# Outputs of four batches in one tile and one store, with loads eight batches ahead

## The chip, the cores and the metric

The kernel runs on one core of one Trainium2 chip. The metric is the time of one execution in device microseconds, as the median of several runs.

## The reference

```python
batch, dim_i, dim_j, dim_k = 32, 256, 512, 384
# x: (batch, dim_i, dim_j) float32, y: (batch, dim_j, dim_k) float32
np.einsum('bij,bjk->bik', x, y).astype(np.float32)
```

There are 32 independent products of a 256 x 512 matrix with a 512 x 384 matrix. For each batch x is 512 KB, y is 768 KB and the output is 384 KB.

## The kernel before

The kernel works through the batches one by one. `load(b)` issues two DMAs on the SyncE queue: x of the batch to `x_sb` (L52), where each of the 128 partitions gets two neighbouring rows of x, one run of 4 KB, and y to `y_sb` (L53), where each partition gets four neighbouring rows of y, one run of 6 KB. `compute(b)` casts y to fp16 in four pieces, two on ScalarE (L61) and two on VectorE (L63). TensorE transposes x in eight pieces of 128 x 128 against an identity (L69), and VectorE and ScalarE take them out of PSUM in fp16 (L71, L73). Eight matmuls of 128 x 128 by 128 x 384 then sum into two PSUM tiles (L82), which ScalarE and VectorE copy to the halves of `o_sb` (L91, L93). `store(b)` issues one DMA on the SyncE queue that writes `o_sb` to the output (L97): each partition holds two neighbouring rows, so it is one run of 3 KB per partition on either side.

The order on the SyncE queue is the order of the program: the loads of batches 0 to 5, and then, for each batch b, the two loads of batch b + 6 and the store of batch b. SyncE issues in that order, so a store that waits for its copies keeps the loads behind it back. Each DMA signals one of eight semaphores in turn, and an issue waits until the DMA eight places before it has landed; at most eight DMAs are in flight. The identity is made on GpSimd after the first two loads in program order. `x_pool` and `y_pool` have AHEAD + 3 = 9 buffers, `o_pool` has 8.

Of the kernel before, what the change touches and what calls it, by code (L numbers as in the profile page):

```python
# [1 line left out]

# [5 lines left out]


MM_DT = mybir.dt.float16  # L10
F32 = mybir.dt.float32
P = 128
AHEAD = 6


@with_exitstack
def kernel(
    ctx: ExitStack,
    tc: tile.TileContext,
    x: bass.AP,  # L20
    y: bass.AP,
    out: bass.AP,
):
    nc = tc.nc

    B, I, J = x.shape
    _, _, K = y.shape

    NI = I // P
    NJ = J // P  # L30

    const_pool = ctx.enter_context(tc.tile_pool(name="const", bufs=1))
    x_pool = ctx.enter_context(tc.tile_pool(name="x_pool", bufs=AHEAD + 3))
    y_pool = ctx.enter_context(tc.tile_pool(name="y_pool", bufs=AHEAD + 3))
    yr_pool = ctx.enter_context(tc.tile_pool(name="yr_pool", bufs=4))
    xt_pool = ctx.enter_context(tc.tile_pool(name="xt_pool", bufs=4))
    o_pool = ctx.enter_context(tc.tile_pool(name="o_pool", bufs=8))
    tpsum_pool = ctx.enter_context(tc.tile_pool(name="tpsum", bufs=4, space=bass.MemoryType.PSUM))
    opsum_pool = ctx.enter_context(tc.tile_pool(name="opsum", bufs=4, space=bass.MemoryType.PSUM))

    identity = const_pool.tile([P, P], F32)

    loaded = {}

    def load(b):


        x_sb = x_pool.tile([P, NI, J], F32, name="x_sb")
        y_sb = y_pool.tile([P, NJ, K], F32, name="y_sb")
        x_src = x[b].rearrange("(p r) j -> p r j", p=P)  # L50
        y_src = y[b].rearrange("(q t) k -> q t k", q=P)
        nc.sync.dma_start(out=x_sb, in_=x_src)  # L52
        nc.sync.dma_start(out=y_sb, in_=y_src)  # L53
        loaded[b] = x_sb, y_sb

    def compute(b):
        x_sb, y_sb = loaded.pop(b)
        y_r = yr_pool.tile([P, NJ, K], MM_DT, name="y_r")
        for t in range(NJ):
            if t % 2 == 0:  # L60
                nc.scalar.copy(y_r[:, t], y_sb[:, t])  # L61
            else:
                nc.vector.tensor_copy(y_r[:, t], y_sb[:, t])  # L63

        xt_sb = xt_pool.tile([P, NJ, NI, P], MM_DT, name="xt_sb")
        for t in range(NJ):
            t_ps = tpsum_pool.tile([P, NI, P], F32, name="t_ps")
            for r in range(NI):
                nc.tensor.transpose(t_ps[:, r], x_sb[:, r, t::NJ], identity)  # L69
            if t % 2 == 0:  # L70
                nc.vector.tensor_copy(xt_sb[:, t], t_ps)  # L71
            else:
                nc.scalar.copy(xt_sb[:, t], t_ps)  # L73

        o_sb = o_pool.tile([P, NI, K], F32, name="o_sb")
        o_ps = [
            opsum_pool.tile([P, K], F32, name=f"o_ps_{r}", tag="o_ps")
            for r in range(NI)
        ]
        for t in range(NJ):  # L80
            for r in range(NI):
                nc.tensor.matmul(  # L82
                    o_ps[r],
                    xt_sb[:, t, r],
                    y_r[:, t],
                    start=(t == 0),
                    stop=(t == NJ - 1),
                )
        for r in range(NI):
            if r % 2 == 0:  # L90
                nc.scalar.copy(o_sb[:, r, :], o_ps[r])  # L91
            else:
                nc.vector.tensor_copy(o_sb[:, r, :], o_ps[r])  # L93
        return o_sb

    def store(b, o_sb):
        nc.sync.dma_start(  # L97
            out=out[b].rearrange("(p r) k -> p r k", p=P), in_=o_sb
        )

    HEAD = 2
    load(0)
    load(1)
    make_identity(nc, identity)
    for b in range(HEAD, AHEAD):
        load(b)
    for b in range(B):
        if b + AHEAD < B:
            load(b + AHEAD)
        store(b, compute(b))  # L110


# [1 line left out]
_INS = ['x', 'y']  # L114
_OUTS = [((32, 256, 384), 'float32')]


# [23 lines left out]
```

## Time and profile before

| | |
|---|---|
| median of 8 runs | 137.18 us (137.09 to 137.43) |
| the profiled execution | 137.23 us, its span 135.5 us |
| busy: PE, PEld, DVE, ACT, POOL | 64%, 44%, 46%, 51%, 1% of the span |
| HBM read and written | 41.94 MB and 12.58 MB, 403 GB/s over the span |
| granted TensorE clock, mean | 0.98 |
| x load: DMAs, KB each, median us from issue to landing | 32, 512, 10.2 |
| y load | 32, 768, 11.2 |
| store | 32, 384, 10.9 |

PE is TensorE's matmul, PEld its weight load, DVE VectorE, ACT ScalarE, POOL GpSimd, and SP SyncE; SPq is SyncE's sequencer, which issues the DMAs. In the rows of 40 slices each digit is the busy share of one slice of 3.39 us in tenths. A line of the timeline gives the start in us, the busy time in us, the engine, the line of the kernel, the operation, what it writes and reads, the count, and in brackets the idle time before it and what ended it. A group's line gives busy us and mean ns of one, then the engine's idle time just before the group's instructions and what ended most of it.

### The profile page before, as it was taken

The page shows a single profiled execution, that of the slowest core. Times are in us where ns is not written, and L with a number is a line of the kernel's source. Part 1 is how long each engine was busy: PE and PEld are TensorE (multiplying, and loading weights), DVE is VectorE, ACT ScalarE, POOL GpSimd, SP SyncE. Part 2 cuts the span into 40 slices and gives each one's busy share as a digit, 9 for nine tenths or more (in the row PEclk, how much of TensorE's full clock was granted, in tenths as well). Part 3 has the DMA queues.
Part 4 walks back from the last instruction along what each step waited for, and adds up shares of the span by engine and source line. Part 5 has one row for each costly group of instructions (what it writes and reads, how often), then busy time and mean ns, then how long its engine had stood idle before and what let it go on. Part 6 is the DMA issues. An engine that isn't in the chain of part 4 may idle for free.

```text
span 135.5 us, 1733 instructions
## 1 busy us (share of the span) xinstructions
PE 86.8 (64%) x512; PEld 60.2 (44%) x512; DVE 62.7 (46%) x160; ACT 68.8 (51%) x161; POOL 0.7 (1%) x6
## 2 busy tenths in 40 slices
PE   0599777777576677555676565676565677565640
PEld 0458555554255455334454344454344454344410
DVE  0247555554155544446454456554446544446520
ACT  3246666663266544546454656454646454546520
POOL 2000000000000000000000000000000000000000
PEclk9999999999689999999999999999999999999997
DMA  4999999999999999999999999999999999999993
GB/s 158 423 416 418 418 414 387 413 417 412 420 422 422 415 417 419 421 417 422 426 415 419 416 426 420 423 420 413 421 423 423 412 419 420 421 418 427 410 379 132
DMA packets 13833, 54.64 MB, mean 403 GB/s; under 512 B 1536, under 2 KB 1536, under 8 KB 13824
## 3 DMA queue, kind: packets, MB, share of 16 engines
q1 hardware_dynamic: 13824, 54.53, 98.7%
q8 instruction: 4, 0.07, 0.2%
q14 instruction: 5, 0.04, 0.1%
HBM read 41.94 MB, written 12.58 MB: 403 GB/s over the span
## 4 chain that ended last, share of the span: by engine, by line
DMA 88%; PE 4%; ACT 2%; issue 1%; SPq 1%; DVE 0%; ACTq 0%
DMA out_dram<-o_sb 33%; DMA y_sb<-in_y_dram 33%; DMA x_sb<-in_x_dram 22%; PE o_ps L82 4%; ACT y_r L61 2%; ACT o_sb L91 1%; DVE o_sb L93 0%; SPq L53 0%; SPq L52 0%; ACTq L61 0%; SPq L97 0%
## 5 line engine op out<-in xcount | busy, mean ns | idle before, releaser
L82 PE MATMUL o_ps<-y_r,xt_sb 128*128 128x384 f16 x256 | 49.5, 337 | 35.3 <-ACT y_r L61 29.8
L82 PEld LDWEIGHTS <-xt_sb 128*128 128x128 f16 x256 | 25.3, 99 | 52.6 <-issue 36.6
L69 PE MATMUL t_ps<-identity,x_sb 128*128 128x128 f32 x256 | 39.3, 298 | 8.1 <-DMA x_sb<-in_x_dram 8.1
L69 PEld LDWEIGHTS t_ps<-identity,x_sb 128*128 128x128 f32 x256 | 35.1, 210 | 17.0 <-PE o_ps L82 12.0
L93 DVE COPY o_sb<-o_ps 128x384 f32<-128x384 f32 x32 | 17.8, 557 | 44.3 <-PE o_ps L82 44.3
L61 ACT CAST y_r<-y_sb 128x384 f16<-128x384 f32 x64 | 29.7, 510 | 13.2 <-DMA y_sb<-in_y_dram 13.1
L73 ACT CAST xt_sb<-t_ps 128x256 f16<-128x256 f32 x64 | 23.6, 372 | 17.7 <-PE t_ps L69 15.2
L91 ACT COPY o_sb<-o_ps 128x384 f32<-128x384 f32 x32 | 15.3, 478 | 30.1 <-PE o_ps L82 30.1
L63 DVE CAST y_r<-y_sb 128x384 f16<-128x384 f32 x64 | 20.0, 355 | 19.7 <-DMA y_sb<-in_y_dram 19.5
L71 DVE CAST xt_sb<-t_ps 128x256 f16<-128x256 f32 x64 | 26.3, 421 | 4.1 <-PE t_ps L69 3.3
L61 ACT ACT_TABLE_LOAD x1 | 1.3, 1283 | 0.7 <-PEq L125 0.7
masks.py:199 POOL TENSOR_SCALAR_AFFINE_SELECT identity<-identity 128x128 f32<-128x128 f32 x1 | 0.3, 292 | 0.1
masks.py:197 POOL MEMSET identity<- 128x128 f32 x1 | 0.2, 204 | 0.3 <-POOLq L125 0.3
L125 POOL MEMSET const-bfloat16-1.0<- 128x1 bf16 x1 | 0.1, 101 | 0.0
L125 POOL MEMSET const-uint8-127<- 128x1 uint8 x1 | 0.1, 101 | 0.0
L125 POOL MEMSET const-float32-0.0<- 128x1 f32 x1 | 0.1, 98 | 0.2 <-issue 0.2
L125 POOL MEMSET const-float32-1.0<- 128x1 f32 x1 | 0.1, 98 | 0.0
## 6 DMA issues: line engine op xcount, KB each, us to landing
y_sb<-in_y_dram SPq DMA_DIRECT2D x32, 768.0 KB, 11.2
x_sb<-in_x_dram SPq DMA_DIRECT2D x32, 512.0 KB, 10.2
out_dram<-o_sb SPq DMA_DIRECT2D x32, 384.0 KB, 10.9
```

The source lines that it names most:

```text
L61: nc.scalar.copy(y_r[:, t], y_sb[:, t])
L63: nc.vector.tensor_copy(y_r[:, t], y_sb[:, t])
L69: nc.tensor.transpose(t_ps[:, r], x_sb[:, r, t::NJ], identity)
L71: nc.vector.tensor_copy(xt_sb[:, t], t_ps)
L73: nc.scalar.copy(xt_sb[:, t], t_ps)
L82: nc.tensor.matmul(o_ps[r], xt_sb[:, t, r], y_r[:, t], start=(t == 0), stop=(t == NJ - 1),)
L91: nc.scalar.copy(o_sb[:, r, :], o_ps[r])
L93: nc.vector.tensor_copy(o_sb[:, r, :], o_ps[r])
L125: nc = _bacc.Bacc("TRN2", target_bir_lowering=False, num_devices=1)
```

## The change

The outputs of several batches in a row share one tile `o_sb` of 128 partitions x n batches x 768 values, with n from the list `GROUPS`: six groups of four, two of two and four of one. A group is stored by one DMA after its last batch. For n over 1 a new function `wide_dma` builds the DMA instruction itself, so that the two sides keep different shapes: on the side of SBUF one run per partition (12 KB for n = 4), on the side of HBM n runs of 3 KB, one in each batch of the output. AHEAD is 8 instead of 6, `x_pool` and `y_pool` have AHEAD + 2 = 10 buffers, and `o_pool` has four for the groups of four and two together and four for the single batches. The identity is made ahead of all loads in program order, and all first loads are issued in one loop. The computation of a batch is the same.

```diff
@@ -10,7 +10,32 @@
 MM_DT = mybir.dt.float16
 F32 = mybir.dt.float32
 P = 128
-AHEAD = 6
+AHEAD = 8
+GROUPS = [4, 4, 4, 4, 4, 4, 2, 2, 1, 1, 1, 1]
+
+
+def wide_dma(eng, out, in_):
+
+    nc = eng.bass
+
+    def side(ap):
+        return [
+            mybir.BassSymbolicTensorAccessPattern(
+                ap=ap.ap, dtype=ap.dtype, bass_ap=ap, is_dma=False
+            )
+        ]
+
+    return eng.add_instruction(
+        mybir.InstDMACopy(
+            name=nc.get_next_instruction_name(),
+            engine=eng.engine,
+            ins=side(in_),
+            outs=side(out),
+            queue="qSPDynamicHW",
+            mode="Copy",
+            cce_op=mybir.AluOpType.bypass,
+        )
+    )
 
 
 @with_exitstack
@@ -30,15 +55,16 @@
     NJ = J // P
 
     const_pool = ctx.enter_context(tc.tile_pool(name="const", bufs=1))
-    x_pool = ctx.enter_context(tc.tile_pool(name="x_pool", bufs=AHEAD + 3))
-    y_pool = ctx.enter_context(tc.tile_pool(name="y_pool", bufs=AHEAD + 3))
+    x_pool = ctx.enter_context(tc.tile_pool(name="x_pool", bufs=AHEAD + 2))
+    y_pool = ctx.enter_context(tc.tile_pool(name="y_pool", bufs=AHEAD + 2))
     yr_pool = ctx.enter_context(tc.tile_pool(name="yr_pool", bufs=4))
     xt_pool = ctx.enter_context(tc.tile_pool(name="xt_pool", bufs=4))
-    o_pool = ctx.enter_context(tc.tile_pool(name="o_pool", bufs=8))
+    o_pool = ctx.enter_context(tc.tile_pool(name="o_pool", bufs=4))
     tpsum_pool = ctx.enter_context(tc.tile_pool(name="tpsum", bufs=4, space=bass.MemoryType.PSUM))
     opsum_pool = ctx.enter_context(tc.tile_pool(name="opsum", bufs=4, space=bass.MemoryType.PSUM))
 
     identity = const_pool.tile([P, P], F32)
+    make_identity(nc, identity)
 
     loaded = {}
 
@@ -47,13 +73,11 @@
 
         x_sb = x_pool.tile([P, NI, J], F32, name="x_sb")
         y_sb = y_pool.tile([P, NJ, K], F32, name="y_sb")
-        x_src = x[b].rearrange("(p r) j -> p r j", p=P)
-        y_src = y[b].rearrange("(q t) k -> q t k", q=P)
-        nc.sync.dma_start(out=x_sb, in_=x_src)
-        nc.sync.dma_start(out=y_sb, in_=y_src)
+        nc.sync.dma_start(out=x_sb, in_=x[b].rearrange("(p r) j -> p r j", p=P))
+        nc.sync.dma_start(out=y_sb, in_=y[b].rearrange("(q t) k -> q t k", q=P))
         loaded[b] = x_sb, y_sb
 
-    def compute(b):
+    def compute(b, o_sb):
         x_sb, y_sb = loaded.pop(b)
         y_r = yr_pool.tile([P, NJ, K], MM_DT, name="y_r")
         for t in range(NJ):
@@ -72,7 +96,6 @@
             else:
                 nc.scalar.copy(xt_sb[:, t], t_ps)
 
-        o_sb = o_pool.tile([P, NI, K], F32, name="o_sb")
         o_ps = [
             opsum_pool.tile([P, K], F32, name=f"o_ps_{r}", tag="o_ps")
             for r in range(NI)
@@ -88,26 +111,30 @@
                 )
         for r in range(NI):
             if r % 2 == 0:
-                nc.scalar.copy(o_sb[:, r, :], o_ps[r])
+                nc.scalar.copy(o_sb[:, r], o_ps[r])
             else:
-                nc.vector.tensor_copy(o_sb[:, r, :], o_ps[r])
-        return o_sb
+                nc.vector.tensor_copy(o_sb[:, r], o_ps[r])
 
-    def store(b, o_sb):
-        nc.sync.dma_start(
-            out=out[b].rearrange("(p r) k -> p r k", p=P), in_=o_sb
-        )
+    def store(b, n, o_sb):
+        dst = out[b : b + n].rearrange("b (p r) k -> p b (r k)", p=P)
+        src = o_sb.rearrange("p b r k -> p b (r k)")
+        if n == 1:
+            nc.sync.dma_start(out=dst[:, 0], in_=src[:, 0])
+        else:
+            wide_dma(nc.sync, dst, src.rearrange("p (o b) q -> p o (b q)", o=1))
 
-    HEAD = 2
-    load(0)
-    load(1)
-    make_identity(nc, identity)
-    for b in range(HEAD, AHEAD):
+    for b in range(AHEAD):
         load(b)
-    for b in range(B):
-        if b + AHEAD < B:
-            load(b + AHEAD)
-        store(b, compute(b))
+    b = 0
+    for n in GROUPS:
+        o_sb = o_pool.tile([P, n, NI, K], F32, name="o_sb", tag=f"o_sb_{min(n, 2)}")
+        for g in range(n):
+            if b + AHEAD < B:
+                load(b + AHEAD)
+            compute(b, o_sb[:, g])
+            b += 1
+        store(b - n, n, o_sb)
+    assert b == B
 
 
 # ---- launch: one core; inputs and outputs as the reference has them ----
```

## The prediction

> **What bounds the kernel now.** I read the page first: the busy rows of the 40 slices, the queue table, the chain. Then the waits of the SyncE queue, then the timeline, and last the trace's records of single DMA packets and of landings (each DMA raises its semaphore sixteen times, once per engine).
>
> ```profile
> DMA  4999999999999999999999999999999999999993
> GB/s 158 423 416 418 418 414 387 413 417 412 420 422 422 415 417 419 421 417 422 426 415 419 416 426 420 423 420 413 421 423 423 412 419 420 421 418 427 410 379 132
> q1 hardware_dynamic: 13824, 54.53, 98.7%
> DMA 88%; PE 4%; ACT 2%; issue 1%; SPq 1%; DVE 0%; ACTq 0%
> L82 PE MATMUL o_ps<-y_r,xt_sb 128*128 128x384 f16 x256 | 49.5, 337 | 35.3 <-ACT y_r L61 29.8
> ```
>
> The sixteen DMA engines are busy from the second slice to the last but one, no compute engine passes 64%, and the chain is 88% DMA. So the time is a start of about 2 us, the service of 54.53 MB, and the last landing. Whatever doesn't alter what the DMA engines do per batch is worth nothing.
>
> The price of a batch comes from the SyncE timeline. Each issue waits for the DMA eight places before it, so it marks a landing.
>
> ```profile
> 9.31 0.33 SPq L53 DMA_DIRECT2D y_sb<-in_y_dram  x1
> ...
> 21.96 0.33 SPq L53 DMA_DIRECT2D y_sb<-in_y_dram  x1
> ...
> 81.76 0.34 SPq L97 DMA_DIRECT2D out_dram<-o_sb  x1
> ...
> 114.15 0.34 SPq L97 DMA_DIRECT2D out_dram<-o_sb  x1
> ```
>
> The issues at 9.31 and 21.96 waited for y of batches 1 and 5, with only loads moving: 12.65 / 4 = 3.16 us for the loads of a batch. From 81.76 to 114.15 eight batches passed with stores between loads: 32.39 / 8 = 4.05 us. A store among loads thus costs 4.05 - 3.16 = 0.89 us. At the end, with no loads left, the stores land on the slowest engine from 129.06 to 134.62: 5.56 / 6 = 0.93 us for a store among stores. So a store between loads hides 0.04 us of itself (0.041 unrounded) under its neighbours.
>
> The packet records give the fixed part. Their medians are 159 ns for a 4 KB run of x, 234 ns for 6 KB of y, 121 ns for 3 KB of the output and 9 ns for a semaphore write. 2 KB more cost 75 ns; take that slope from 159 and 9 ns remain, the price of the empty semaphore record too. A record is 9 ns plus 37.5 ns per KB. But records overlap: a store has 8 on each engine and a semaphore, 8 x 121 + 9 = 977 ns, and lands every 927. Of that 8 x 112.5 = 900 is bytes, so 27 ns over nine records, 3 ns each, is what the fixed part really costs when stores follow each other.
>
> **The change, part by part.**
>
> *Fewer records.* Six groups of four go from 512 read runs to 128, two groups of two from 256 to 128: 6 x 384 + 2 x 128 = 2,560 fewer, 160 on each engine. DMAs that store go from 32 to 12, so 20 semaphore writes fewer per engine: 180 records. No row shows a 12 KB read beside four 3 KB writes. The upper bound is the whole fixed part, 180 x 9 = 1.62 us saved; the lower bound is that the write side, which keeps its 3 KB pieces, sets the pace, and 20 x 3 ns = 0.06 us is saved. I take 3 ns, because it is measured between stores: 180 x 3 = 0.54 us saved.
>
> The Trainium skill (DMA: Bandwidth & Descriptors, "Why small descriptors are slow (HBM only)") speaks against the change: it puts a fixed overhead of about three cycles on a packet and says that joining descriptors is only worth it up to 256 B. The rows, 3 ns beside 116 ns of a 3 KB store run, leave the same little; by the rule taken strictly the saving would be 0 and the sum 138.0.
>
> *Fewer borders between loads and stores.* Before, 25 stores have loads behind them (stores 0 to 24); after, five blocks have (groups 0 to 4; the sixth store follows the last load). If the hidden 0.041 us belongs to a border, 20 of them are lost: 20 x 0.041 = 0.82 us. If it goes with the bytes, nothing is lost. I take 0.82: an engine's ring is served in order, so a load can only overlap the store next to it.
>
> The same page ("Where 436 GB/s comes from") gives a ceiling of 435 GB/s, 0.904 us for the bytes of one store. The row of 0.89 is already under that and the one of 0.93 just above; by the ceiling the 28 grouped stores could save 28 x 0.023 = 0.64 us at most, and the sum with the borders would be 137.4.
>
> *Loads eight ahead.* SyncE still waits for the DMA eight places back at each issue; in the changed program too the ninth DMA waits on the first's semaphore. So the depth in flight doesn't grow with AHEAD; only its bytes do, where a store is 1.5 MB. With the rings never empty, that is worth 0. A load now takes the buffer of ten batches before instead of nine; SyncE's wait for L69 was 0.7 us in total. The cover is the queue of seven DMAs, some 10 us; if it went, each late us would be a us of the end.
>
> *Stores moved back in SyncE's queue.* The first store comes after the loads of batch 11 instead of batch 6, and each grouped store waits for the copies of its fourth batch, with eight load issues of the next group behind it. Those copies must be done when the x load four batches later has landed. Compute, when its data is there, takes 3.28 us a batch:
>
> ```profile
> 17.09 1.46 PE L82 MATMUL o_ps<-y_r,xt_sb 128*128 128x384 f16 x8 [0.87 <-DVE y_r L63]
> ...
> 20.37 1.46 PE L82 MATMUL o_ps<-y_r,xt_sb 128*128 128x384 f16 x8 [0.87 <-DVE y_r L63]
> ...
> 35.26 1.12 PE L82 MATMUL o_ps<-y_r,xt_sb 128*128 128x384 f16 x3 [2.39 <-ACT y_r L61]
> ```
>
> Four batches compute in 13.1 us and arrive in 16.2. The third line is the risk: after 2.39 us of idle time eight matmuls ran at half the granted clock (the 6 in PEclk). A block of stores leaves PE idle up to 3.6 us, so each group may pay once; doubling one batch's 86.8 / 32 = 2.7 us still fits in the 3.1 us to spare. Cost 0. Built, PE, DVE, ACT and POOL hold the same instructions in the same order as before, the identity on POOL included. An issue of a wide store takes between 0.34 and, at four times the runs, 1.4 us of a queue that waits most of the time: 0.
>
> *The end.* Twelve batches of stores follow the last load, not seven, so the chain from last load through compute to last store (issue at 130.87, landing 134.6) is covered on every engine. Before, only the faster engines ran dry; the slowest landed a store every 0.93 us to the end. I take 0; the bound is the loss in slice 39, (420 - 379) / 420 x 3.39 = 0.33 us gained.
>
> **Sum.** -0.54 + 0.82 = +0.28 us on the profiled execution's 137.23 (135.5 span and 1.7 around it): 137.51. The median of the runs is 0.05 lower, so 137.45. Runs of this kernel spread so that 0.2%, 0.27 us, is what a measurement can tell; the forecast stands on that line. Own range 136.9 to 137.65: the overlap lost by half to wholly, the record at 2 to 4 ns (-0.31 to +0.46).
>
> **Rivals.**
>
> *Faster: the read run pays the whole fixed part.* Then 1.62 us go: 135.56, or 136.38 with the borders lost; I say 136.0. For it: all four sizes lie on one line with 9 ns, and 12 KB would be 459 ns instead of 4 x 121 = 484. Against it: the windows show a DMA share of 1.02 to 1.04, so records overlap, and 977 became 927. It decides where over 5 ns a record are saved.
>
> *Slower: the write side sets the pace.* Four 3 KB writes cost as four records did and the borders are lost: +0.82 - 0.06 = +0.76, 137.95. Long runs of loads may add: between 12 and 21 us, with loads alone, records rose to 162.4 and 238.6 ns on average, 8 x (3.4 + 4.6) = 64 ns a batch, though the landings kept 3.16 us; a sixth of that over 32 batches is 0.3 us, 138.25. It decides where less than 1.5 ns a record is saved.
>
> *The form doesn't do what it says.* If the queue cuts the read to 3 KB as well, the records stay and only borders and semaphores count: again 137.95.
>
> **How the numbers follow.** Forecast 0.40 (faster 0.05, same 0.20, slower 0.15), faster rival 0.32, slower rival 0.20 (0.02 of it same), uncut form 0.08. Faster 0.37, same 0.22, slower 0.41. The range leaves out the fullest saving, below 135.8, and the worst long runs, above 138.25.
>
> **What would show it.** On the page: the records of queue q1 fall from 13,824 by 2,560 + 320 to 10,944 if a wide run is one record; stay at 13,504 if not. Store to store on SyncE, a group's period before is 16.20 us. The forecast is 4 x 3.162 + 4 x 0.927 - 27 x 0.003 - 0.041 = 16.24, the faster rival's 15.95 to 16.08, the slower rival's 16.31. Wrong altogether would be SyncE waiting for ACT or DVE before a wide store, a DMA digit under 9 within the span, or a load period other than 3.16 us.

## The result and the profile after

The changed kernel takes 137.94 us (median of 12 runs, 137.76 to 138.4) where the kernel before takes 137.22 (35 runs): a ratio of 1.0053, 95% interval 1.0043 to 1.0064. It is slower by some 0.7 us. The profiled execution took 137.98 us with a span of 136.1.

The rows of the changed kernel's page that answer to those shown of before are these.

```profile
PEclk9999999999999975579999999999757999999975
DMA  4999999999999999999999999999999999999991
GB/s 169 413 418 421 416 416 416 412 406 418 410 436 398 418 418 416 439 402 424 416 415 434 412 418 411 415 435 406 422 416 431 415 414 418 409 430 415 413 383 61
q1 hardware_dynamic: 10944, 54.53, 97.9%
DMA 61%; PE 16%; DVE 10%; ACT 2%; SPq 2%; issue 1%; ACTq 0%
```

The DMA engines are still the bound: nines from the second slice to the last but one. The records of queue q1 fell to 10,944, the number that the prediction gave for one record per wide run, so the DMA does what its instruction says. The wide record has a median of 466 ns in the trace (the line of the other sizes gave 459). PEclk now drops twice within the run, for 10.2 and 6.8 us, each time behind a block of stores that had left TensorE idle (before, once for 3.4 us), and again at the end, where TensorE has no work left in either kernel; the DMA row stays at nine through it. The chain is of little use here: it ends at the last compute instruction, and the stores behind that have become longer.

The timeline of SyncE gives the pace of a group: the first load behind each wide store.

```profile
47.70 0.55 SPq L28 DMA_DIRECT2D out_dram<-o_sb  x1
49.60 0.34 SPq L76 DMA_DIRECT2D x_sb<-in_x_dram  x1
...
98.29 0.33 SPq L76 DMA_DIRECT2D x_sb<-in_x_dram  x1
```

From 49.60 to 98.29 three groups passed: 48.69 / 3 = 16.23 us each. The forecast was 16.24 (its own terms add up to 16.23), before it was 16.20. So the steady part costs 0.03 us a group, and that is not enough for the result. An issue of a wide store took 0.55 us of SyncE instead of 0.34.

None of the signs came by which the prediction would have been wrong altogether. The DMA digits stay at nine, and inside a group the loads of a batch still follow each other at 3.1 to 3.2 us (49.60 above, then 52.75 and 55.91). In front of each of its eight issues of wide stores SyncE waited for a load (us in total, times, longest):

```profile
SPq L28 <- DMA x_sb<-in_x_dram: 7.0, 7, 1.9
SPq L28 <- DMA y_sb<-in_y_dram: 1.3, 1, 1.3
```

The same list names a copy to `o_sb` (L114, L116) in front of none of them; only the fourth, at 80.58, went out 0.4 us after its wait for the load had ended.

The waits of SyncE show the second difference. The line of the closing waits of the kernel before comes first, that of the changed kernel after it (us in total, times, longest).

```profile
SPq L136 <- DMA out_dram<-o_sb: 3.2, 4, 0.9
```

```profile
SPq L163 <- DMA out_dram<-o_sb: 7.6, 1, 7.6
```

At its end SyncE waits for the eight DMA semaphores, in a fixed order. Before, the last store had the eighth of them (96 DMAs, a multiple of eight), and the last waits ended one by one as the last stores landed. After, the last store has the fourth (76 DMAs): SyncE stands 7.6 us in front of that one, and then still has four waits to go through that have long been fulfilled. In the trace these follow the last landing (135.04) at steps of 0.066 us. From the last landing to the end of the span there are 1.09 us, where before there were 0.83.

### The profile page after: what moved, and what is told of

Its sections match the earlier page's. It is cut to its first block, busy times and chain, and to the rows that moved or that the text cites. A ratio compares the mean times of both kernels' runs of the same rounds, so it can differ in the third digit from the quotient of the medians.

```text
span 136.1 us, 1658 instructions
## 1 busy us (share of the span) xinstructions
PE 87.6 (64%) x512; PEld 63.8 (47%) x512; DVE 57.9 (43%) x160; ACT 66.6 (49%) x161; POOL 0.7 (1%) x6
## 3 DMA queue, kind: packets, MB, share of 16 engines
q1 hardware_dynamic: 10944, 54.53, 97.9%
## 4 chain that ended last, share of the span: by engine, by line
DMA 61%; PE 16%; DVE 10%; ACT 2%; SPq 2%; issue 1%; ACTq 0%
DMA y_sb<-in_y_dram 40%; DMA x_sb<-in_x_dram 21%; PE o_ps L105 13%; DVE xt_sb L95 5%; DVE y_r L87 4%; PE t_ps L93 4%; ACT y_r L85 1%; SPq L76 1%; DVE o_sb L116 1%; SPq L77 1%; ACT xt_sb L97 1%; ACT o_sb L114 0%; ACTq L85 0%
## 5 line engine op out<-in xcount | busy, mean ns | idle before, releaser
L105 PE MATMUL o_ps<-y_r,xt_sb 128*128 128x384 f16 x256 | 52.1, 350 | 27.4 <-DVE y_r L87 18.3
L105 PEld LDWEIGHTS <-xt_sb 128*128 128x128 f16 x256 | 26.2, 103 | 46.7 <-issue 28.9
L93 PE MATMUL t_ps<-identity,x_sb 128*128 128x128 f32 x256 | 40.5, 307 | 11.4 <-DMA x_sb<-in_x_dram 11.4
L93 PEld LDWEIGHTS t_ps<-identity,x_sb 128*128 128x128 f32 x256 | 37.7, 210 | 15.6 <-issue 12.1
L116 DVE COPY o_sb<-o_ps 128x384 f32<-128x384 f32 x32 | 17.8, 557 | 49.8 <-PE o_ps L105 49.8
L114 ACT COPY o_sb<-o_ps 128x384 f32<-128x384 f32 x32 | 15.3, 478 | 32.4 <-PE o_ps L105 32.4
L95 DVE CAST xt_sb<-t_ps 128x256 f16<-128x256 f32 x64 | 24.7, 416 | 9.0 <-PE t_ps L93 8.9
```

The costliest lines, as they stand in the source:

```text
L105: nc.tensor.matmul(o_ps[r], xt_sb[:, t, r], y_r[:, t], start=(t == 0), stop=(t == NJ - 1),)
L114: nc.scalar.copy(o_sb[:, r], o_ps[r])
L116: nc.vector.tensor_copy(o_sb[:, r], o_ps[r])
```

## The experiments

The first theory was the prediction's: each border between stores and loads that is lost costs 0.04 us, a run that isn't read on its own saves some ns, nothing else counts. Its rivals were the depth of the loads, the wide form itself, and, after the first four runs, the closing waits. Each kernel's time is a median; ratios are to the kernel before on the same chip.

**Loads eight ahead, stores as before.**

```diff
-GROUPS = [4, 4, 4, 4, 4, 4, 2, 2, 1, 1, 1, 1]
+GROUPS = [1] * 32
-    o_pool = ctx.enter_context(tc.tile_pool(name="o_pool", bufs=4))
+    o_pool = ctx.enter_context(tc.tile_pool(name="o_pool", bufs=8))
```

> Stores of single batches as before (32 DMAs of 384 KB), but loads eight ahead, ten load buffers and the identity ahead of the loads, as in the changed kernel. Theory of the borders (each border between a store and loads that is lost costs 0.04 us, nothing else counts): 24 stores have loads behind them instead of 25, so 137.25 us, a batch every 4.05 us. Theory of the depth (loads eight ahead are what costs): 137.9 us, as the changed kernel. Theory of the wide form (a DMA of 1.5 MB or its 12 KB runs cost): 137.2 us.

Measured 137.31 us, ratio 1.0002 (0.9990 to 1.0015). The depth, the buffers and the place of the identity cost nothing that can be measured. The whole loss lies in the grouped stores and in what comes with them, fewer DMAs included. (Of the stores in this kernel 23 have loads behind them, not 24 as expected; by the theory that is 0.04 us.)

**Groups of four, but 3 KB runs on both sides.**

```diff
-            wide_dma(nc.sync, dst, src.rearrange("p (o b) q -> p o (b q)", o=1))
+            nc.sync.dma_start(out=dst, in_=src)
```

> The changed kernel with the same groups and one DMA per group, but cut to 3 KB runs on the side of SBUF too. Theory of the borders with the pace set by bytes and the write side: the read run is worth nothing, 137.95 us, a block of four lands in 3.7 us, as with 12 KB runs. Theory that 12 KB runs save their share (3 ns a record, 24 records a block): 0.07 us a block slower than the changed kernel, 138.4 us in all. Theory that 12 KB runs themselves are slow (466 ns a record where the line gave 459): 0.05 us a block faster, 137.6 us.

Measured 138.55 us, ratio 1.0085 (1.0063 to 1.0107). This is slower than the changed kernel by 0.6 us in the medians, 0.4 by the two ratios. So the wide run does save, which the theory of the write side had excluded. The two intervals just touch; the landings below give the same size.

**Groups of four, four stores one behind the other.**

```diff
-            wide_dma(nc.sync, dst, src.rearrange("p (o b) q -> p o (b q)", o=1))
+            for g in range(n):
+                nc.sync.dma_start(out=dst[:, g], in_=src[:, g])
```

> The changed kernel with the same groups in one tile, but each batch of a group stored by its own DMA, all of a group one behind the other after its last batch. Theory of the borders: as the changed kernel plus 20 semaphore writes, 137.95 to 138.1 us. Theory of the size (one DMA of 1.5 MB among the eight in flight, or its form, costs): back to 137.2 us.

Measured 138.51 us, ratio 1.0089 (1.0066 to 1.0111). Putting the stores of four batches behind one another costs 1.2 us against single stores (137.31), with the very same DMAs. It is not the size of a DMA. Nor did the DMA engines run dry behind stores that wait for compute: this kernel's DMA row has nines from the second slice to the last but one.

**Wide groups, loads six ahead.**

```diff
-AHEAD = 8
+AHEAD = 6
```

(with nine load buffers)

> The changed kernel with loads six ahead and nine load buffers. Theory of the borders: six blocks have loads behind them instead of five, 137.9 us. Theory of the depth: 137.2 us, as before.

Measured 138.14 us, ratio 1.0072 (1.0045 to 1.0099): not the depth, again.

The traces of these kernels split the loss. The landing of the last store is an increment for each of sixteen engines; its mean and its last tell what an average engine had to do, and how far the slowest was behind.

| kernel | mean engine's last landing, us | slowest behind the mean, us | last landing to end of span, us |
|---|---|---|---|
| single stores, eight ahead | 133.30 | 1.15 | 0.83 |
| four stores behind one another | 134.10 | 1.68 | 0.83 |
| one DMA, 3 KB runs | 134.08 | 1.66 | 1.09 |
| the changed kernel | 133.43 | 1.61 | 1.09 |

Grouping costs the mean engine 0.80 us. Twenty semaphore writes fewer save it 0.02, the wide runs 0.65. On top of that the slowest engine is 0.5 us further behind in the three kernels that group, and the closing waits add 0.26 where the last store is not on the last semaphore. (These are single executions; that of the single stores was 0.25 us under its median. In the kernel before and in the wide groups with loads six ahead, the faster engines wait for the last store at the end, so their means don't compare.)

The packet records show where the 0.80 sits. With four stores behind one another a record of x took 162.3 ns on average, one of y 237.7 and one of the output 121.8; with single stores 161.15, 236.1 and 121.4. An engine has 256 of each (4,096 by sixteen), which makes 0.31, 0.41 and 0.09 us: nine tenths of the loss is in the records of the loads and not of the stores. In the prediction's window with loads alone they were as long (162.4 and 238.6).

The 0.5 us is the difference of one execution of each kernel. Read while all engines still have work, at about 130 us, the slowest engine is 1.6 to 1.9 us behind in every trace with groups of four stored in a row and in that of the groups of two, and 1.0 to 1.5 with single stores, halves or quarters between the loads; the kernel before has 1.4 there, and the groups of eight, whose DMA engines run dry a little later, 1.2. So the direction holds, and the size is uncertain.

**Four small DMAs more, in the changed kernel and in the one before.** In each, behind the loads of batch 1:

```diff
+    pad = const_pool.tile([1, 4], F32, name="pad")
+    for i in range(4):
+        nc.sync.dma_start(out=pad[0:1, i : i + 1], in_=x[0, 0:1, i : i + 1])
```

> The changed kernel with four more DMAs of 4 bytes each, behind the loads of batch 1, so that the count of DMAs is 80 instead of 76 and the last store uses the last of the eight semaphores. In the runs so far SyncE ends by waiting for the eight semaphores in their fixed order; where the last store is on the fourth, four more waits of 0.066 us follow its landing (0.27 us), where it is on the eighth, none. Theory of the closing waits: 137.7 us, 0.25 less than the changed kernel, and one wait behind the last landing. Theory that all of the loss is in the service of the DMA engines: 137.95 us.

> The kernel before with the same four small DMAs: 100 DMAs instead of 96, the last store on the fourth semaphore. Theory of the closing waits: 137.5 us, 0.27 more than before, with five waits behind the last landing. Rival: 137.25 us.

Measured 137.83 us (1.0046, 1.0034 to 1.0058) and 137.77 us (1.0039, 1.0026 to 1.0052). The last landing came 0.17 us later in the one and 0.28 in the other. With the closing waits that makes 0.17 - 0.26 = -0.09 us for the changed kernel (the medians: -0.11, not to be told from nothing by the intervals) and 0.28 + 0.26 = 0.54 for the kernel before (the medians: 0.52). Whether the later landing is the price of the small DMAs was not tried by itself. The place where it belongs shows it whole: from the last landing to the end of the span the changed kernel with 80 DMAs has 0.83 us instead of 1.09, the kernel before with 100 DMAs 1.09 instead of 0.83. The closing wait of the latter now reads like that of the changed kernel:

```profile
SPq L139 <- DMA out_dram<-o_sb: 3.4, 1, 3.4
```

**12 KB runs on both sides.**

```diff
-            wide_dma(nc.sync, dst, src.rearrange("p (o b) q -> p o (b q)", o=1))
+            flat = out[b : b + n].rearrange("b i k -> (b i k)")
+            nc.sync.dma_start(
+                out=flat.rearrange("(p q) -> p q", p=P),
+                in_=src.rearrange("p b q -> p (b q)"),
+            )
```

> The changed kernel with stores whose runs are 12 KB on both sides: each partition's 12 KB goes to one run of the output, so the values lie elsewhere in it; bytes, groups and borders are the same. From cutting the read side to 3 KB the kernel lost 0.6 us. Theory that the fixed part is paid for each run that is read, whatever the write: 137.95 us, as the changed kernel, a block of four in 3.7 us. Theory that the written runs pay too: about 0.6 us less, 137.3 us. For the sum of the prediction, which put the fixed part on the read side: 137.95 us.

Measured 137.84 us, ratio 1.0039 (1.0025 to 1.0052), 0.1 less than with 3 KB writes; the two intervals overlap. In the traces the mean engine's last landing came 0.21 us earlier than in the changed kernel (133.22), where the wide read had gained 0.65, and a record of 12 KB took 460 ns (median) instead of 466. So most of the fixed part is paid on the read side; the times alone don't show that the written runs pay at all.

**Stores in two halves, one between the x load and the y load** (in the kernel before).

```diff
         nc.sync.dma_start(out=x_sb, in_=x_src)
+        if between is not None:
+            store(*between, 1)
...
+        dst = out[b].rearrange("(p two r) k -> two p r k", two=2, r=NI)
+        nc.sync.dma_start(out=dst[half], in_=o_sb[half:P:2])
```

> The kernel before with each store cut into two DMAs, of the even and of the odd partitions: one goes out behind the two loads, the other between the x load and the y load of the next step. Records and bytes are as before, 32 semaphore writes an engine more, and the blocks of stores between loads are doubled from 25 to 50. Theory of the borders (0.06 us for each block lost, from the runs so far): 25 x 0.06 = 1.5 us gained, 32 x 0.01 lost, 136.1 us, a batch every 4.0 us. Theory that it is the grouping in itself and not the border that costs: 137.2 + 0.3 = 137.5 us. If 64 partitions are read more slowly: 138 us and more.

Measured 137.05 us, ratio 0.9988 (0.9979 to 0.9997). An expectation that failed: it gained 0.2 us, not 1.1. A batch took 4.05 us as before (landings of the first halves on the slowest engine). So a border has no fixed price: 25 more of them, at the cost of 32 more semaphore writes, gave next to nothing. Why was not tried.

**Groups of two.**

```diff
-GROUPS = [4, 4, 4, 4, 4, 4, 2, 2, 1, 1, 1, 1]
+GROUPS = [2] * 12 + [4, 2, 1, 1]
```

> The changed kernel with groups of two (the last eight batches 4, 2, 1, 1), 80 DMAs, so no waits behind the last landing. Against single stores eight ahead (137.31 us), by the runs so far: theory of an even price for each store that is joined (grouping 0.06 lost, DMA 0.012 and run 0.03 saved): 12 x 0.06 - 16 x 0.042 = +0.05, 137.35 us. Theory that any grouping brings the late engines a fixed loss of some 0.8 us: 137.31 + 0.8 + 12 x 0.02 - 0.67 = 137.7 us.

Measured 137.15 us, ratio 0.9996 (0.9984 to 1.0008): no difference. The fixed loss of 0.8 us for any grouping is out; the even price gave 137.35, so twelve borders fewer cost less than that. (Its one profiled execution took 137.63, almost 0.5 us over the median, so its mean landing is not set beside the others.)

**Groups of eight.**

```diff
-GROUPS = [4, 4, 4, 4, 4, 4, 2, 2, 1, 1, 1, 1]
+GROUPS = [8, 8, 8, 2, 2, 2, 1, 1]
-    o_pool = ctx.enter_context(tc.tile_pool(name="o_pool", bufs=4))
+    o_pool = ctx.enter_context(tc.tile_pool(name="o_pool", bufs=2))
```

> The changed kernel with groups of eight (24 KB runs read), then 2, 2, 2, 1, 1: 72 DMAs, no waits behind the last landing. Even price: 22 blocks between loads less than with single stores, 22 x 0.06 - 24 x 0.042 = +0.3, 137.6 us. Fixed loss: 137.31 + 0.8 + 22 x 0.02 - 1.0 = 137.55 us. Theory that the length of the runs of loads is what costs: 138.2 us or more.

Measured 141.61 us, ratio 1.0321 (1.0300 to 1.0343), and none of the theories: it is another mechanism.

```profile
DMA  4999999999999999989999999989999999995556
```

```profile
SPq L28 <- DVE o_sb L116: 21.5, 2, 17.4
```

The DMA row falls to fives at the end, and SyncE stood 17.4 us before a wide store whose copies were not done. The likely reason, not tried by itself, is that with two output buffers the small last groups share their slots with the large ones and wait for their landing, so that compute ran late. The wait came behind the last load, whose issue was at 107.50, with nothing but stores left in the queue. So it says nothing on the length of the runs of loads; it shows what it costs when the DMA engines do run dry.

**Stores alone.** No loads and no arithmetic; a tile of zeros is stored to the 32 batches in four forms.

```diff
+    for b in range(8):
+        narrow(b)
+    wide(8); wide(12)
+    fused(16); fused(20)
+    both(24); both(28)
```

> No loads and no arithmetic: a tile of zeros is stored to the 32 batches, eight narrow stores, two wide ones of four batches, two of four batches with 3 KB runs on both sides, two with 12 KB runs on both sides. It measures the prices by themselves. By the prediction's terms, per four batches: narrow 4 x 0.927 = 3.71 us, one DMA with 3 KB runs 3.70, wide 3.63 (24 records at 3 ns less), both sides wide the same. Theory that joined runs save nothing where stores follow stores: 3.70 for all.

Landings on the slowest engine, per four batches: narrow 4.00 us (seven stores in 7.01), one DMA with 3 KB runs 3.91, wide 3.78, both sides wide 3.71. By these means each step of joining saves something, the wide run 0.12 us over 24 records, 5 ns each. But there are two landings of each joined form, and the two of one form lie up to 0.15 us apart (wide 3.86 and 3.71), so only the order is to be read from them. A narrow store alone took 1.00 us, more than the 0.89 among loads; its record was 124 ns instead of 121.

**12 KB runs, but the stores spread between the loads.** Each group of four is stored in four DMAs of every fourth partition, one behind the loads of each of the next four batches.

```diff
-GROUPS = [4, 4, 4, 4, 4, 4, 2, 2, 1, 1, 1, 1]
+GROUPS = [4] * 7 + [3, 1]
...
+    def store_part(b, n, o_sb, j):
+        dst = out[b : b + n].rearrange("b (p four r) k -> four p b (r k)", four=4, r=NI)
+        src = o_sb[j:P:4].rearrange("p b r k -> p (b r k)")
+        wide_dma(nc.sync, dst[j], src.rearrange("p (o q) -> p o q", o=1))
...
                 load(b + AHEAD)
+                if parts is not None:
+                    store_part(*parts, g)
```

> The changed kernel, but each group of four that has loads behind it is stored in four DMAs of every fourth partition, one behind the loads of each of the next four batches; the last twelve batches are stored in groups of four, four, three and one, so that 88 DMAs end on the eighth semaphore. Runs are 12 KB read, 3 KB written, and a batch's worth of store lies between any two batches' loads, as in the kernel before. Theory that grouping costs by long runs of loads and of stores while the 12 KB runs save 0.6 us wherever they stand: 136.7 us, faster than both kernels. Theory that 12 KB runs save only inside long blocks of stores, where a narrow store lands in 0.927 us and not in 0.886: 137.2 us. If reading 32 partitions spread like this is slower: above 137.5 us.

Measured 136.90 us, ratio 0.9968 (0.9957 to 0.9979): faster than both kernels, though 0.2 short of the first theory and 0.3 under the second. It keeps the short runs of loads and a store's worth between any two batches' loads, and it ends on the eighth semaphore (88 DMAs).

```profile
PEclk9999999999999999999999999999999999999855
DMA  4999999999999999999999999999999999999992
q1 hardware_dynamic: 10752, 54.53, 98.3%
```

Fewer records than the changed kernel, and the clock of TensorE no longer drops until its work is done; no block of stores leaves it idle. The mean engine's last landing is 133.06, 0.37 before that of the changed kernel and 0.24 before that of single stores, and the slowest is 1.16 us behind it, as with single stores (1.15) and not 1.61. An engine has 192 records fewer than with single stores, so 0.24 us (0.41 by the medians) is 1 to 2 ns a record: spread between loads, the wide runs save about half of what they save in blocks, or less.

## Why the prediction was right

The time lies in the wide range of forecast and rivals together, on the side that had the largest chance. The forecast itself was missed: its sum gave 137.45 and its own range ended at 137.65, 0.3 us short. By its value the result is the slower rival's 137.95, and that is luck: the rival's first reason, the pace of the write side, is not the cause, and the two terms left out, 0.26 us of closing waits and some 0.5 us of a later slowest engine, stand in no one's sum. (The 0.041 of the prediction is 0.040 from its lines unrounded, which alters nothing.)

*Fewer records: right, and a little small.* 160 read runs and 20 semaphores were to save 0.54 us on each engine. The mean engine's landings give 0.65 + 0.02, some 4 ns a run. The count of records was exact. That the read side pays was right for the most part; the slower rival, by which the written pieces set the pace, fell with the narrow groups (138.55) and the writes of 12 KB (137.84).

The rule of the Trainium skill that was weighed (DMA: Bandwidth & Descriptors, "Why small descriptors are slow (HBM only)"), that joining is only worth it up to 256 B, is not borne out in the strict reading that the prediction gave it: at 3 KB joining gave 0.65 us of 137, small but above what a measurement can tell. The page says it of putting consecutive descriptors into one packet; here the runs themselves became longer, so its sentence as it stands was not tried. Another section of that page, "Rules for kernel authors", asks for at least 1 MiB a DMA: one DMA of 1.5 MB in place of four of 384 KB gave 138.55 against 138.51 us here, with 0.26 of the former being closing waits.

*Borders: right in size, not as a rule.* Forecast 0.82 us, measured 0.80 on the mean engine. That they agree so well is in part luck, for a price for each border doesn't carry over: with stores in halves 25 borders more brought 0.2 us, with groups of two twelve fewer lost nothing that could be measured. The records put the loss into the loads, which run longer where no store stands among them; the slower rival had named this ("long runs of loads"), with 0.3 us for it.

*Loads ahead, SyncE's queue, TensorE's clock: 0, as said.* Single stores eight ahead made no difference; the clock did fall after blocks of stores, for longer than the one batch that was reckoned with, and compute had the time. What a queue that runs dry costs, the groups of eight show: 4.4 us.

*The end: wrong.* It was put at 0 with a bound of 0.33 us to be gained. The term left out is SyncE's closing waits: the count of DMAs went from a multiple of eight to four beyond one, and 0.26 us of waits came behind the last landing. The list of SyncE's waits showed them in the profile of before; they were not counted for the new number of DMAs.

*The sum went by one engine.* The forecast reckoned what an engine has to do and left the slowest as far behind as it was. Grouped, it is half a us further behind its mean in the executions of the table: 1.61 to 1.68 us in the three kernels that group, 1.15 and 1.16 where a store stands between any two loads. With these two terms the account for the profiled executions closes, as it must, since the terms are differences of the same landings: 0.13 for the mean engine (0.80 - 0.02 - 0.65), 0.46 for the slowest, 0.26 of closing waits and 0.07 outside the span make 0.92, from 137.06 to 137.98 us; the medians differ by 0.63, since that execution of the single stores was a quick one. Why the slowest engine falls further behind is open. The trace has four instruction loads of 16 KB, each a record of about 1 us, and five records of 8 KB. The first step of its lateness goes with the first of the 16 KB: in the traces of nine kernels it grew by 0.9 to 1.5 us right there, at 25 to 35 us, in single and in grouped kernels alike (0.62 to 1.56 in the changed one). A second step, 1.56 to 2.05 in the changed kernel by 47.6 us, comes around the first grouped store, in the kernels that store groups of four or of two in a row (0.2 to 0.8 us) and not in that with groups of eight. In the changed kernel two 8 KB records are near, but with loads six ahead and with groups of two it had come by 37 us, 9 us before them. So these loads alone don't explain the difference; the records carry no engine, and no run here took the loads away.

## What to carry to other kernels

Where the DMA engines are the bound, joining runs on the side that is read saves a few ns a run, but gather the runs without gathering the transfers: with a store's worth between any two batches' loads a gain was left (136.90 us), four stores in a row lost it. Count what the last instruction of a queue still has to walk through behind the last landing: here a DMA count that is no multiple of the eight semaphores cost 0.26 us. And reckon for the slowest engine, not for a typical one: what it came later, some 0.5 us, was as large as the terms of the sum.

## What the runs showed of the hardware

Fulfilled waits at the end of SyncE's queue cost 0.066 us each. With four more DMAs of 4 bytes the last landing came 0.17 and 0.28 us later, in one execution each. Stores with no loads beside them ran slower than among loads: 1.00 us a batch alone, 0.93 behind the last loads, 0.89 among them. And the sixteen engines part by up to 2.9 us over 135 us (first to last landing of the last store). A record of a load took 1.2 to 1.6 ns longer, of 161 and 236, where the stores came four in a row than where one stood between any two loads.
